# Holding the first four output stores of a convolution until the middle of the third image pair

## The chip, the cores and the metric

The kernel runs on one core of a Trainium2 chip. The metric is the device time of one execution in microseconds (us); the kernel is launched once for the whole computation. Lower is better.

## The reference

A 3x3 convolution with zero padding of 1, stride 1, in fp32, over 16 images of 64 channels and 64 x 64 pixels, to 128 output channels. The weights are given with nine tenths of their values at zero, but the kernel treats them as dense.

```python
def reference(x, weight):               # x (16, 64, 64, 64), weight (128, 64, 3, 3), float32
    ...
    x_pad = np.pad(x, ((0, 0), (0, 0), (pad, pad), (pad, pad)), mode='constant')
    output = np.zeros((batch, c_out, h, w), dtype=np.float32)
    ...
        output[b, co] += weight[co, ci, kh, kw] * x_pad[b, ci, kh:kh+h, kw:kw+w]
    ...
```

The output, 16 x 128 x 64 x 64 floats, is 33.55 MB; the input is 16.78 MB in fp32.

## The kernel before

**Tiling.** The 16 images are taken as 8 pairs. A pair lies on 128 partitions (two images of 64 channels each) as a bf16 tile `xs[p]` of 64 x 64 pixels. One output image is a tile `o` of 128 partitions (its output channels) by 64 x 64 fp32, that is 16 KB for each partition and 2 MB in all. For each pair there are two of them, `o[0]` and `o[1]`.

**Loads.** SyncE issues the load of the weights (L60) and of the upper half of the first pair in fp32 (L62, into a tile of the output pool). GpSimd issues the lower half of the first pair (L63) and the seven other pairs (L67). These eight convert from fp32 to bf16 on the way, so a whole pair writes 1 MB (it reads 2 MB). All are issued within the first 6.2 us, one behind another on GpSimd's queue.

**Compute.** A pair is four blocks of 16 output rows (`blk` 0 to 3). A block goes through `twos` (L151): GpSimd adds neighbouring rows of `xs[p]` into `s` (L154), TensorE forms a shared product of it that ScalarE copies from PSUM to `pc` (L161), TensorE forms a product for the even rows and one for the odd rows (`product`, L121 to L142), and VectorE adds each to `pc` and writes the rows into `o[0]` and `o[1]`: four `tensor_tensor` instructions for each block (L168). The first block of the first pair goes through `direct` (L144) instead.

**Stores.** After the four blocks of a pair SyncE issues its two stores of 2 MB, `o[0]` first (L188). In the last pair it issues stores of half an image (1 MB) after `blk` 1 and after `blk` 3 (L185). So there are 14 stores of 2 MB and four of 1 MB, all on SyncE's queue and in the order of the program; they are called store 0 to store 17 below. SyncE waits at each one until VectorE has written its tile.

**Buffers.** `o_pool` has 7 buffers that are handed out in turn: one to the fp32 half of the first input pair, then two for each output pair. The third pair takes the sixth and the seventh; the fourth pair takes the first (long free) and the second, which held the first pair's `o[0]`. VectorE must therefore see store 0 landed before it writes `o[1]` of the fourth pair, stores 1 and 2 before the fifth pair, stores 3 and 4 before the sixth, and so on.

**Order.** The program is scheduled by hand (`tc.manual_schedule()`), so each engine runs its instructions in the order in which the code writes them. Semaphore waits are derived from what reads and writes the tiles.

Of the kernel before, what the change touches and what calls it, by code (L numbers as in the profile page):

```python
# [27 lines left out]
def kernel(  # L28
# [6 lines left out]
    nc = tc.nc  # L35

    B, C_IN, H, W = x.shape
# [83 lines left out]
    def product(terms, rows):  # L121


        ps = [psum_pool.tile([128, rows, W], FP32, name="ps") for _ in range(2)]
        todo = [(t, kw) for t in terms for kw in KW_ORDER]
        for i, ((src, g, first, step), kw) in enumerate(todo):
            n_src = src.shape[1]
            lo = 0 if first >= 0 else 1
            hi = rows if first + (rows - 1) * step < n_src else rows - 1
            c_lo, c_hi = max(0, 1 - kw), min(W, W + 1 - kw)  # L130
            a = first + lo * step
            b = first + (hi - 1) * step + 1
            for n in range(2):
                q = slice(64 * n, 64 * n + 64)
                nc.tensor.matmul(  # L135
                    ps[n][:, lo:hi, c_lo:c_hi],
                    tap(g, kw, n),
                    src[q, a:b:step, c_lo + kw - 1 : c_hi + kw - 1],
                    start=(i == 0),
                    stop=(i == len(todo) - 1),  # L140
                )
        return ps  # L142

    def direct(p, o, r0, rows):  # L144
        ps = product(
            [(xs[p], G1, r0, 1), (xs[p], G0, r0 - 1, 1), (xs[p], G2, r0 + 1, 1)], rows
        )
        nc.scalar.copy(out=o[0][:, r0 : r0 + rows, :], in_=ps[0])  # L148
        nc.vector.tensor_copy(out=o[1][:, r0 : r0 + rows, :], in_=ps[1])  # L149

    def twos(p, o, r0):  # L151
        t0 = r0 // 2
        s = s_pool.tile([128, 8, W], BF16, name="s")
        nc.gpsimd.tensor_tensor(  # L154
            out=s, in0=xs[p][:, r0 : r0 + 16 : 2, :], in1=xs[p][:, r0 + 1 : r0 + 16 : 2, :], op=ADD
        )
        shared = product([(s, G1, 0, 1)], 8)
        pc = []
        for n in range(2):
            c = p_pool.tile([128, 8, W], FP32, name="pc")  # L160
            nc.scalar.copy(out=c, in_=shared[n])  # L161
            pc.append(c)
        even = [(xs[p], G21, r0 + 1, 2), (xs[p], G0, r0 - 1, 2)]
        odd = [(xs[p], G01, r0, 2), (xs[p], G2, r0 + 2, 2)]
        for first, terms in ((r0, even), (r0 + 1, odd)):
            ps = product(terms, 8)
            for n in range(2):
                nc.vector.tensor_tensor(  # L168
                    out=o[n][:, first : r0 + 16 : 2, :], in0=ps[n], in1=pc[n], op=ADD
                )  # L170

    for p in range(NP):
        o = [o_pool.tile([C_OUT, H, W], FP32, name="o") for _ in range(2)]
        last = p == NP - 1
        for blk in range(4):
            r0 = 16 * blk
            if BLOCKS[p][blk] == "T":
                twos(p, o, r0)
            else:
                for r, rows in ((r0, 8), (r0 + 8, 8)):  # L180
                    direct(p, o, r, rows)
            if last and blk % 2 == 1:
                for n in range(2):
                    rows = slice(r0 - 16, r0 + 16)
                    nc.sync.dma_start(out=out[2 * p + n][:, rows, :], in_=o[n][:, rows, :])  # L185
        if not last:
            for n in range(2):
                nc.sync.dma_start(out=out[2 * p + n], in_=o[n])  # L188


# [28 lines left out]
```

## Time and profile before

| | |
|---|---|
| time, median of 7 runs | 127.67 us |
| lowest and highest of the 7 | 127.62 and 128.13 us |
| the profiled execution's own time | 128.13 us |
| its span in the profile | 126.3 us (126.28 in the trace) |
| DMA moved | 42.93 MB, mean 340 GB/s |
| TensorE busy | 110.3 us (87%) |
| VectorE busy | 82.4 us (65%) |
| GpSimd, ScalarE busy | 40.8 us (32%), 39.0 us (31%) |

The profile is of the slowest of the seven runs: its span is 1.85 us shorter than its time (start and end of the execution lie outside it), and its time is 0.46 us above the median. Times in the text are us from the start of the span. The page cuts the span into 40 slices of 3.16 us; "DMA" is the mean busy share of the 16 DMA engines in tenths, and "GB/s" is what they moved, counted by the bytes written, so that the converting loads appear at half of what they read. "q1 hardware_dynamic" is the queue that SyncE issues on, "q0 software_dynamic" GpSimd's. Under the DMA view the trace holds one record for each packet (start, duration, queue, size). A 2 MB store is 128 packets of 16 KB, eight for each DMA engine, and each engine ends its part with a packet of 4 bytes that raises the semaphore; a store has landed when the last of the 16 has.

### The profile page before, as it was taken

What the parts mean: (1) busy time and instruction counts of PE and PEld (TensorE: products, weight loads), DVE (VectorE), ACT (ScalarE), POOL (GpSimd) and SP (SyncE); (2) the same over time, 40 slices, a digit from 0 to 9 for tenths busy, and PEclk for the clock granted to TensorE, in tenths of its full rate; (3) what the DMA queues carried; (4) which work ended last, traced back from release to release, by engine and by line L of the source; (5) the groups of instructions that cost most, each with busy time, mean ns of one, the idle gap of its engine ahead of it and who ended that gap; (6) DMA issues with size and microseconds to landing.
All of it is one profiled execution on the core that took longest, in us unless ns stands there. A gap on an engine that the chain in (4) does not pass through costs nothing.

```text
span 126.3 us, 2486 instructions
## 1 busy us (share of the span) xinstructions
PE 110.3 (87%) x1002; PEld 56.5 (45%) x1002; DVE 82.4 (65%) x135; ACT 39.0 (31%) x71; POOL 40.8 (32%) x45
## 2 busy tenths in 40 slices
PE   6649999999999999999999999999999999991000
PEld 6414454555455455545554455545554555540000
DVE  0451267787778777877787778777877787776000
ACT  4541232333333333333333333333333333330000
POOL 6909033333333333333333333333333330000000
PEclk9999999999999999999999999999999999999955
DMA  4999999999999999999999999999999979999990
GB/s 114 355 231 210 215 213 213 223 200 252 314 337 298 314 350 301 332 332 413 413 441 441 420 426 415 436 431 418 441 420 426 441 306 426 446 397 407 418 387 23
DMA packets 4044, 42.93 MB, mean 340 GB/s; under 512 B 448, under 2 KB 448, under 8 KB 704
## 3 DMA queue, kind: packets, MB, share of 16 engines
q1 hardware_dynamic: 2880, 34.90, 66.0%
q0 software_dynamic: 1152, 7.86, 30.5%
q8 instruction: 8, 0.13, 0.4%
q14 instruction: 4, 0.03, 0.1%
HBM read 17.07 MB, written 33.55 MB: 401 GB/s over the span
## 4 chain that ended last, share of the span: by engine, by line
PE 83%; DMA 5%; DVE 1%; issue 1%; DVEq 0%; SPq 0%
PE ps L135 83%; DMA o<-in_x_dram 5%; DVE o L168 1%; DVEq L214 0%; DVE x L87 0%; SPq L60 0%; DVEq L168 0%
## 5 line engine op out<-in xcount | busy, mean ns | idle before, releaser
L135 PE MATMUL ps<-x,wT 64*128 64x504 bf16 (+3 forms) x780 | 91.3, 382 | 2.5 <-DVE x L87 2.5
L168 DVE TENSOR_TENSOR o<-ps,pc 128x512 f32<-128x512 f32 x124 | 77.8, 686 | 22.1 <-PE ps L135 19.8
L135 PEld LDWEIGHTS <-wT 64*128 64x128 bf16 x966 | 52.9, 96 | 55.5 <-issue 5.8
L154 POOL TENSOR_TENSOR s<-x 128x512 bf16<-128x512 bf16 x31 | 35.7, 1154 | 61.4 <-PE ps L135 46.4
L161 ACT COPY pc<-ps 128x512 f32<-128x512 f32 x62 | 33.3, 589 | 64.0 <-issue 61.8
L135 PE MATMUL ps<-s,wT 64*128 64x512 bf16 (+1 forms) x186 | 25.5, 377 | 0.0
L149 DVE COPY o<-ps 128x512 f32<-128x512 f32 x2 | 1.4, 692 | 4.7 <-PE ps L135 4.7
L74 PE MATMUL ps<-idle_rhs 128*128 128x128 bf16 x27 | 3.1, 313 | 1.0 <-DVE idle_rhs L71 1.0
L67 POOL DMA_DIRECT2D x<-in_x_dram x7 | 3.7, 560 | 0.0
L74 PEld LDWEIGHTS <-idle_rhs 128*128 128x128 bf16 x27 | 2.8, 149 | 1.0 <-DVE idle_rhs L71 1.0
L91 DVE CAST w_bf<-w_sb 128x192 bf16<-128x192 f32 (+1 forms) x4 | 1.3, 381 | 3.0 <-DMA w_sb<-in_weight_dram 3.0
L148 ACT COPY o<-ps 128x512 f32<-128x512 f32 x2 | 1.2, 586 | 5.2 <-PE ps L135 5.2
L87 DVE CAST x<-o 128x576 bf16<-128x576 f32 x1 | 0.5, 460 | 2.5 <-DMA o<-in_x_dram 2.5
L87 ACT CAST x<-o 128x576 bf16<-128x576 f32 (+1 forms) x2 | 1.5, 802 | 1.5 <-DMA o<-in_x_dram 1.5
L97 PE MATMUL ps<-ident,w_bf 128*128 128x128 bf16 x9 | 1.2, 308 | 0.4 <-DVE w_bf L91 0.4
L91 ACT ACT_TABLE_LOAD x1 | 1.3, 1283 | 0.7 <-PEq L203 0.7
L91 ACT CAST w_bf<-w_sb 128x64 bf16<-128x64 f32 (+1 forms) x2 | 0.7, 417 | 1.9 <-DMA w_sb<-in_weight_dram 1.9
L97 PEld LDWEIGHTS <-w_bf 128*128 128x128 bf16 x9 | 0.8, 130 | 0.8 <-DVE w_bf L91 0.8
L101 DVE TENSOR_TENSOR wT<-ps,wT 128x384 bf16<-128x384 f32 x2 | 1.0, 548 | 0.0
L63 POOL DMA_DIRECT2D x<-in_x_dram x1 | 0.7, 698 | 0.8 <-POOLq L203 0.8
L71 DVE MEMSET idle_rhs<- 128x64 uint32 x1 | 0.1, 112 | 0.8 <-PEq L203 0.8
L110 ACT CAST wT<-ps 128x384 bf16<-128x384 f32 x1 | 0.5, 479 | 0.4 <-PE ps L97 0.4
(8 smaller groups left out, 2.0 us busy)
## 6 DMA issues: line engine op xcount, KB each, us to landing
out_dram<-o SPq DMA_DIRECT2D x14, 2048.0 KB, 16.5
x<-in_x_dram POOLq DMA_DIRECT2D x7, 1024.0 KB, 25.0
out_dram<-o SPq DMA_DIRECT2D x4, 1024.0 KB, 9.4
o<-in_x_dram SPq DMA_DIRECT2D x1, 1024.0 KB, 6.5
x<-in_x_dram POOLq DMA_DIRECT2D x1, 512.0 KB, 7.9
w_sb<-in_weight_dram SPq DMA_DIRECT2D x1, 288.0 KB, 3.1
```

The lines of the kernel that those rows point to most:

```text
L67: nc.gpsimd.dma_start(out=xs[p], in_=pair(p))
L74: nc.tensor.matmul(idle_ps, idle_rhs, idle_rhs, start=True, stop=True)
L87: copy(out=xs[0][:, a:b, :], in_=x_head[:, a:b, :])
L91: copy(out=w_bf4[:, g, a:b, :], in_=w_v[:, k : k + b - a, :])
L97: nc.tensor.matmul(wps[:, j, :], src, ident, start=True, stop=True)
L101: nc.vector.tensor_tensor(out=wT[:, g], in0=wps, in1=wT[:, G1], op=SUB)
L135: nc.tensor.matmul(ps[n][:, lo:hi, c_lo:c_hi], tap(g, kw, n), src[q, a:b:step, c_lo + kw - 1 : c_hi + kw - 1], start=(i == 0), stop=(i == ...
L148: nc.scalar.copy(out=o[0][:, r0 : r0 + rows, :], in_=ps[0])
L149: nc.vector.tensor_copy(out=o[1][:, r0 : r0 + rows, :], in_=ps[1])
L154: nc.gpsimd.tensor_tensor(out=s, in0=xs[p][:, r0 : r0 + 16 : 2, :], in1=xs[p][:, r0 + 1 : r0 + 16 : 2, :], op=ADD)
L161: nc.scalar.copy(out=c, in_=shared[n])
L168: nc.vector.tensor_tensor(out=o[n][:, first : r0 + 16 : 2, :], in0=ps[n], in1=pc[n], op=ADD)
```

## The change

The stores of the first two pairs (stores 0 to 3, `HELD = 2`) are not issued after their pairs. They are kept in a list, and are issued in a row after `blk` 1 of the third pair. Store 0 is given a dependency on the last VectorE instruction of that block (`done`, which `twos` now returns); stores 1 to 3 follow it on SyncE's queue and have nothing more to wait for. All later stores stay where they were. The stores go through a helper `store`, which changes nothing in them. No instruction on TensorE, VectorE, ScalarE or GpSimd is added, removed or moved, and SyncE has the same 18 stores in the same order: only the wait ahead of store 0 differs, and stores 1 to 3 come free with it.

```diff
             for n in range(2):
-                nc.vector.tensor_tensor(
+                done = nc.vector.tensor_tensor(
                     out=o[n][:, first : r0 + 16 : 2, :], in0=ps[n], in1=pc[n], op=ADD
                 )
+        return done
+
+    HELD = 2
+    held = []
+
+    def store(p, n, o, a, b):
+        return nc.sync.dma_start(out=out[2 * p + n][:, a:b, :], in_=o[n][:, a:b, :])
...
             if BLOCKS[p][blk] == "T":
-                twos(p, o, r0)
+                done = twos(p, o, r0)
...
             if last and blk % 2 == 1:
                 for n in range(2):
-                    rows = slice(r0 - 16, r0 + 16)
-                    nc.sync.dma_start(out=out[2 * p + n][:, rows, :], in_=o[n][:, rows, :])
-        if not last:
+                    store(p, n, o, r0 - 16, r0 + 16)
+            if p == HELD and blk == 1:
+                first = store(*held[0])
+                tc.add_manual_dep(
+                    first.ins,
+                    done.ins.name,
+                    mybir.DependencyInfo(
+                        mybir.DependencyClass.Sync, mybir.DependencyReason.DATA
+                    ),
+                    reason="loads first",
+                )
+                for args in held[1:]:
+                    store(*args)
+        if p < HELD:
+            held += [(p, n, o, 0, H) for n in range(2)]
+        elif not last:
             for n in range(2):
-                nc.sync.dma_start(out=out[2 * p + n], in_=o[n])
+                store(p, n, o, 0, H)
```

## The prediction

> **What bounds the kernel now.** I read the chain of waits first. It gives TensorE 83% of the span, and it would make the change harmless, since no instruction of TensorE moves. But the last work of TensorE ends at 114.2 and VectorE's at 115.5, while the span is 126.28. So I read the rows of the page on the DMA engines next.
>
> ```profile
> PE   6649999999999999999999999999999999991000
> ...
> DMA  4999999999999999999999999999999979999990
> GB/s 114 355 231 210 215 213 213 223 200 252 314 337 298 314 350 301 332 332 413 413 441 441 420 426 415 436 431 418 441 420 426 441 306 426 446 397 407 418 387 23
> ...
> q1 hardware_dynamic: 2880, 34.90, 66.0%
> q0 software_dynamic: 1152, 7.86, 30.5%
> ```
>
> The engines are busy in every slice from the second to the 39th, with one dent (the 33rd, 306 GB/s, at 101 to 104). The two queues together take 96.5% of 16 engines' span. There are three phases: loads alone at about 215 GB/s up to 28; loads and stores in turn at 300 to 350 up to 57; stores alone at 413 to 441 after that. The windows say the same: a DMA share of 1.0 or slightly more in the long stretches (neighbouring packets overlap a little).
>
> ```profile
> 8.00:28.00 20.00, 19.82 (x162) 9.51 (x163) 11.91 (x21) 6.64 (x12) 7.98 (x7) 1.00 1.05 216
> 30.00:57.00 27.00, 27.00 (x256) 13.59 (x254) 21.44 (x35) 8.59 (x16) 9.24 (x8) 1.00 1.02 322
> 58.00:100.00 42.00, 42.00 (x397) 21.12 (x394) 32.66 (x52) 14.30 (x27) 15.35 (x14) 1.00 1.01 428
> 100.00:104.00 4.00, 4.00 (x42) 2.10 (x40) 3.16 (x6) 1.08 (x3) 1.35 (x2) 1.00 0.81 340
> ```
>
> The last two columns are the DMA share and GB/s. Next I asked the DMA view for single stores, by a window around the issue of each; the last column is us from issue to landing. Here are stores 0, 3, 5, 9, 11, 12 (issued at 25.40, 38.74, 51.55, 77.16, 89.96, 102.17):
>
> ```profile
> out_dram<-o SPq DMA_DIRECT2D x1, 2048.0 KB, 15.7
> out_dram<-o SPq DMA_DIRECT2D x1, 2048.0 KB, 26.2
> out_dram<-o SPq DMA_DIRECT2D x1, 2048.0 KB, 23.1
> out_dram<-o SPq DMA_DIRECT2D x1, 2048.0 KB, 17.2
> out_dram<-o SPq DMA_DIRECT2D x1, 2048.0 KB, 14.7
> out_dram<-o SPq DMA_DIRECT2D x1, 2048.0 KB, 7.6
> ```
>
> The stores stand in a backlog that shrinks from 26 us to 7.6. Is it gone at 102.17, so that compute sets the end? On most engines, yes; on one, no. The packet records show 14 or 15 engines passing from one 2 MB store to the next in 4.862 us (eight 16 KB packets of 0.611). They run dry between 101.5 and 103.1, and that is the dent. One engine, A from here on, needs 5.165 in the stores-only phase (packets of 0.634 to 0.660). The 4-byte packets that end its part stand at 88.664, 93.840, 98.988, 104.165, 109.323, 114.471. Store 12 was issued at 102.17, so A never waits for work. It ends at 124.72, the other engines mostly at 122.9, and store 17 lands at 125.13. So what sets the end is engine A, busy without a pause since the first loads. Any time in which A stands still is added to the kernel; TensorE has slack beside it.
>
> **The change part by part.**
>
> *When the held stores start.* The release is the last VectorE instruction of block 1 of the third pair:
>
> ```profile
> 42.55 2.52 DVE L168 TENSOR_TENSOR o<-ps,pc 128x512 f32<-128x512 f32 x4 [0.73 <-PE ps L135]
> 45.79 2.51 DVE L168 TENSOR_TENSOR o<-ps,pc 128x512 f32<-128x512 f32 x4 [0.73 <-PE ps L135]
> 49.03 2.48 DVE L168 TENSOR_TENSOR o<-ps,pc 128x512 f32<-128x512 f32 x4 [0.73 <-PE ps L135]
> ```
>
> The third pair's `o[0]` is issued at 50.95, within the last row, so the last row is block 3 and the first is block 1: it ends at 45.07. SyncE issues 0.10 later (as at 25.40, after a tile done at 25.30), at 45.17. From issue to first packet the rings need 0.83 where they are empty (store 12: 102.17 to 103.00) and 4.06 where loads stand in front (store 0 today: 25.40 to 29.46). I take 0.83, because the loads are over by then (next step): first packet at 46.00. With 1.01, as at the weights' load (0.74 to 1.75), it would be 46.18.
>
> *When the loads end.* Alone on the engines, one pair takes 4.867 us of each (4-byte packets of one engine at 12.766, 17.633, 22.500). The third of the 1 MB loads ends between 22.50 and 23.66, depending on the engine; four more take 19.47 and end between 41.97 and 43.13. No engine has anything to do from then until 46.00: 2.9 to 4.0 us of standstill, where today there is none. This is the cost of the change.
>
> *What the separation gives back.* Today four loads and three stores (x 4.867 + 4.862 = 34.05 in all) take A and its peers from 22.5 to 23.7 up to 57.7 to 59.1, 35.3: 1.2 too long, most of it around 27 to 29.5, where load packets take 0.7 to 1.4 instead of 0.624. That 1.2 is saved. But beside loads A's store packets took 0.624 like all others', and its extra 0.3 for each store shows only where stores are alone. In the changed kernel stores 0 to 2 are alone too: 3 x 0.303 = 0.9 comes back as a loss on A.
>
> *The sum on A.* Three stores end at 46.00 + 3 x 5.165 = 61.50; today A has ended store 2 at 57.72. From there on its work is the same: 3.78 later to the end, 128.50, landing at 128.91. On the other engines: 46.00 + 14 x 4.862 + 4 x 2.45 = 123.9, or 124.8 at the 4.93 that a 2 MB store takes after the restart at 103 (107.92 to 112.85), so they don't set the end.
>
> *Who waits for the later landing.* VectorE needs store 0 for the second instruction of the fourth pair, at 52.11 + 0.63 = 52.74. Store 0 would end on A at 51.17 and land 0.37 later, at 51.5 (today the last 4-byte packet is at 40.73 and the landing at 41.10): 1.2 of margin, so it costs nothing. The fifth pair, at about 65, needs stores 1 and 2 (61.9), the sixth, at 77.7, stores 3 and 4 (72.2), the seventh, at 90.5, stores 5 and 6 (82.5): free as well. Without that cover, a landing late by d stalls VectorE by d less 1.2, and TensorE a little later when PSUM is full; even then A has work until 108, 6 us past the time when stores 12 and 13 are issued, so a stall of up to 5 us of TensorE wouldn't reach the end. Behind the waiting store on SyncE's queue are only stores 1 to 3, free with it, and stores 4 and 5, whose tiles are ready at 50.95 and later. GpSimd's loads were all issued by 6.2. No queue is held up that someone else waits on.
>
> *Two rules against rows.* The Trainium skill, "DMA: Bandwidth & Descriptors", in "Anatomy of one DMA", gives the time of a transfer as 2.0 us plus its bytes at 436 GB/s (a fit for GpSimd's path). By this estimate the 33.55 MB of stores end at 45.17 + 2.0 + 77.0 = 124.2, 1.0 before today's landing; the trace has 5.165 for 2 MB on the engine that ends last, where this rule has 4.81, and the trace decides. The same page, in "Latency and other measured facts", says that engines 7 and 15 are usually slower, with GpSimd's descriptor rings as the best guess and as a matter of that path alone. Here the slow engine is slow from 58 to 114, when GpSimd's queue moves nothing, and not while it loads; if the rule did hold, A would lose nothing on stores and the end would be that of the other engines.
>
> **The rivals.** (1) *Forecast: standstill plus A's pace*: +3.78. The profiled span becomes 130.06 and its time 131.91; the median of the seven runs is 0.46 below the profiled one, so 131.45, given as 131.4. (2) *A's slowness is not of stores alone but of today's mix* and it runs like the rest. Then the end is that of 16 equal engines: 46.00 + 14 x 4.862 + 4 x 2.45 + 0.41 = 124.3 at the fast pace, 0.8 before 125.13, that is 126.8 and faster; at 4.93 for a store it is 125.2, no change, 127.8. It decides if a 2 MB store costs A less than (125.13 - 0.41 - 46.00 - 10.25) / 14 = 4.89 (10.25 is A's time for the last four today). Against it: eleven stores at 5.13 to 5.18 in a row, through dent and restart; for it: its packets were normal in the mix and nearly so in the last 1 MB stores (2.45). (3) *A loses less*: 5.0 for a store gives 2.3 less on 14, +1.5, 129.1. (4) *The restart is slow* or store 0 lands too late: 4.06 instead of 0.83 adds 3.2, 134.6; only loads in front of it explain the 4.06, so little is left for it. (5) *The change doesn't do what it says*: if the wait were passed earlier, the stores would start among the loads as today and the time would be 127.7.
>
> **How the numbers follow.** A measurement of this kernel can tell about 0.2% (0.26 us) from no change. Forecast 0.78 (130.4 to 132.2, from an A of 5.10 to 5.18 and a start 0.2 earlier or later); (3) 0.12, spread over 128.1 to 130.4; (2) 0.06, split between faster 0.03 and same 0.03; (4) 0.03; (5) 0.01, same. So faster 0.03, same 0.04, slower 0.93. The range leaves out the lower half of (3), (2), (5) and (4): 129.3 to 132.4.
>
> **What would show it.** In the changed profile: the slices near 42 to 46 fall well below 9 in the DMA row, with q0 empty after about 43.5; 215 GB/s up to there; no slice at 300 to 350; no dent at 101 to 104; the 4-byte packets of one engine 5.1 to 5.2 apart from the first store on; VectorE's idle time and TensorE's end (114.2) unchanged; store 17 landing near 128.9. It would be wrong if all 16 engines end together near 124, if the loads run past 45, or if VectorE waits on a DMA in the fourth pair.

## The result and the profile after

| | before | after |
|---|---|---|
| median | 127.68 us (34 runs) | 129.29 us (13 runs) |
| lowest and highest | 127.10 and 130.03 | 127.60 and 130.61 |
| profiled execution: time, span | 128.13, 126.28 | 129.51, 127.7 |

The change makes the kernel slower: the ratio is 1.0092, with a 95% interval of 1.0068 to 1.0116. The ratio leaves out runs over 1.5% above the fastest of their kernel, five of the change's among them, so it is smaller than that of the medians (1.0126, 1.61 us); the runs of the change spread over 3 us, and why they do is part of the explanation. The forecast of 131.4 had the direction right and the size more than twice too large, and the median lies 0.01 us under the range.

The rows of the page on TensorE, the DMA engines and the two queues, for the changed kernel (a slice is 3.19 us):

```profile
PE   6569999999999999999999999999999999920000
...
DMA  4999999999999499999999999999999999999970
GB/s 133 342 223 213 218 218 215 210 218 221 210 213 218 131 410 410 410 472 410 413 410 421 462 416 410 416 418 441 421 421 421 416 446 426 421 392 418 426 313 18
...
q1 hardware_dynamic: 2880, 34.90, 65.4%
q0 software_dynamic: 1152, 7.86, 29.6%
```

The middle phase at 300 to 350 GB/s is gone: loads alone up to the 13th slice, at 210 to 223 from the third on, then stores alone. Between them stands one slice at 131 GB/s and a busy share of 4, and the dent before the last stores is gone. The windows put the standstill in place; the last two columns are the DMA share and GB/s:

```profile
42.00:43.00 1.00, 1.00 (x12) 0.57 (x10) 1.00 (x3) 0.11 (x1) 0.01 (x1) 1.00 0.26 57
43.00:44.40 1.40, 1.40 (x18) 0.70 (x13) 0.67 (x2) 0.97 (x2) 1.15 (x1) 1.00 0.00 0
44.40:46.00 1.60, 1.60 (x18) 0.88 (x16) 1.60 (x3) 0.00 (x0) 0.00 (x0) 1.00 1.18 492
```

The timeline shows the start of TensorE's real work, the block that releases the stores, and the release:

```profile
7.66 5.67 PE L135 MATMUL ps<-x,wT 64*128 64x512 bf16 x36 [2.51 <-DVE x L87]
...
40.97 2.52 DVE L168 TENSOR_TENSOR o<-ps,pc 128x512 f32<-128x512 f32 x4 [0.73 <-PE ps L135]
...
43.58 3.09 SPq L179 DMA_DIRECT2D out_dram<-o  x4
```

Block 1 of the third pair ends at 43.49, not 45.07, and SyncE issues store 0 at 43.58; the packet records have the first store packet at 44.42. The answers of the DMA view for store 0 (43.58) and store 12 (issued at 100.60):

```profile
out_dram<-o SPq DMA_DIRECT2D x1, 2048.0 KB, 6.4
...
out_dram<-o SPq DMA_DIRECT2D x1, 2048.0 KB, 11.3
```

Store 0 lands in 6.4 us instead of 15.7, since no loads stand in front of it. Store 12 needs 11.3 instead of 7.6: at its issue more of the earlier stores still stand in front of it. The last store lands at 126.60.

### The profile page after: what moved, and what is told of

The parts are those of the page before. It is cut to its first block, busy times and chain, and to the rows that moved or that the text cites. A ratio compares the mean times of both kernels' runs of the same rounds, so it can differ in the third digit from the quotient of the medians.

```text
span 127.7 us, 2486 instructions
## 1 busy us (share of the span) xinstructions
PE 108.9 (85%) x1002; PEld 58.8 (46%) x1002; DVE 82.3 (64%) x135; ACT 39.0 (31%) x71; POOL 40.8 (32%) x45
## 4 chain that ended last, share of the span: by engine, by line
PE 81%; DMA 5%; DVE 1%; issue 1%; DVEq 0%; SPq 0%
PE ps L135 81%; DMA o<-in_x_dram 5%; DVE o L168 1%; DVEq L236 0%; DVE x L87 0%; SPq L60 0%; DVEq L168 0%
## 5 line engine op out<-in xcount | busy, mean ns | idle before, releaser
L135 PEld LDWEIGHTS <-wT 64*128 64x128 bf16 x966 | 55.4, 95 | 51.8 <-issue 4.1
```

The costliest lines, as they stand in the source:

```text
L135: nc.tensor.matmul(ps[n][:, lo:hi, c_lo:c_hi], tap(g, kw, n), src[q, a:b:step, c_lo + kw - 1 : c_hi + kw - 1], start=(i == 0), stop=(i == ...
```

## Experiments

In the packet records I read two numbers for each kernel: the first store packet, and the landing of the last store. Theory "standstill" is the forecast's: the time is the release plus what the slow DMA engine needs for all stores, and only the standstill costs.

**Release after block 0.**

```diff
-            if p == HELD and blk == 1:
+            if p == HELD and blk == 0:
```

> The held stores are released after block 0 of the third pair instead of block 1. In the profile of the change block 0 ends 3.24 us before block 1, at about 40.4, while the loads end on the engines between 42.0 and 43.5. Theory standstill (the DMA engines stood still from 42.0-43.5 to 44.4, and the time is the release plus the stores on the slowest engine): no engine stands still, so the time falls by the 1.0 to 2.4 us of the standstill, to 126.9-128.3, about the kernel before (127.7) or a little under it; the DMA row of the page has no slice below 9 at 40 to 46. Rival pace (what costs is that stores run alone, so that one engine needs 5.14 us for each where it needed 4.99 beside loads): a release 3.2 us earlier changes hardly anything in that, the stores still run almost alone, and the time stays within 0.5 us of 129.3.

Measured: median 127.50 us (12 runs, 127.10 to 128.37), ratio to before 0.9987 (0.9969 to 1.0006). The rows of its page:

```profile
DMA  4999999999999999999999999999999999999960
GB/s 138 344 227 214 208 216 216 222 216 214 208 216 216 334 425 433 417 433 427 440 417 438 417 422 443 427 433 420 422 422 443 396 427 433 427 388 420 422 261 13
```

No slice below 9, and the loss is gone, while loads and stores are nearly as separate as in the change: the rate goes from 216 GB/s to 425 with a single mixed slice, of 334, between them. So it isn't the separation that costs.

**Release after block 2.**

```diff
-            if p == HELD and blk == 1:
+            if p == HELD and blk == 2:
```

> The held stores are released after block 2 of the third pair, 3.24 us later than in the change, at about 46.8. Theory standstill: the end follows the release one for one, 129.3 + 3.2 = 132.5 us. Store 0 then lands at about 47.7 + 5.14 + 0.4 = 53.2 where VectorE needs it at 51.2, so VectorE stalls for 2 us on a DMA in the fourth pair and TensorE ends up to 2 us later, without any further effect on the end because the stores have a backlog. Rival compute (the end is set by the fourth pair being held up, or by the last stores being issued late): the end follows the stall of VectorE only, about +2 us over a kernel with no stall, 130 to 131.5. Rival pace: under 0.5 us of change, 129.3 to 129.8.

Measured: median 131.87 us (6 runs, 130.44 to 132.96), ratio 1.0285 (1.0235 to 1.0334). That is 2.6 us over the change's median, not the full 3.2; the release of the profiled execution was at 44.76, only 1.18 after that of the change's profile, since its first 36 matmuls ended 2.06 earlier (they started at 7.28 and took 3.99, where the change's started at 7.66 and took 5.67), and that execution took 130.51, 1.00 more than the change's. What VectorE waited for, and its timeline at the fourth pair:

```profile
DVE o L168 <- DMA out_dram<-o: 2.8, 2, 2.1
```

```profile
48.48 0.69 DVE L168 TENSOR_TENSOR o<-ps,pc 128x512 f32<-128x512 f32 x1 [0.60 <-PE ps L135]
51.30 6.67 DVE L168 TENSOR_TENSOR o<-ps,pc 128x512 f32<-128x512 f32 x11 [2.14 <-DMA out_dram<-o]
```

The second instruction of the pair waits 2.14 us for store 0, which landed at 51.18. It then catches up with eleven instructions in a row, and VectorE ends at 112.30, before the change's 113.97. The stall is there and costs nothing at the end, as the backlog covers it.

**One store not held.**

```diff
         if p < HELD:
-            held += [(p, n, o, 0, H) for n in range(2)]
+            if p == 0:
+                store(p, 0, o, 0, H)
+            held += [(p, n, o, 0, H) for n in range(2) if (p, n) != (0, 0)]
```

> Store 0 is issued after the first pair as in the kernel before; stores 1 to 3 are held as in the change. Store 0 gives each DMA engine 4.9 us of work among the loads, so the loads end at about 47-48.5 instead of 42.0-43.5, past the release at 43.6. Theory standstill: no engine stands still, and the time falls by 1.0 to 2.4 us, to 126.9-128.3. Rival pace: stores 1 to 17 still run without loads beside them but for the first, so at most 0.3 us is saved and the time is 129.0-129.3. If stores among loads cost more than they save (in the kernel before, loads and three stores took 1.2 us longer together than one by one), the time is nearer 128.3 than 126.9.

Measured: median 128.03 us (12 runs, 127.73 to 128.35), ratio 1.0025 (1.0010 to 1.0040). The loads end between 49.1 and 52.6, no slice of the DMA row between the first and the 39th is below 9, and most of the loss is gone. What is left, 0.3 us, is at the end of the interval that the expectation gave to loads and stores costing more together.

**Stores cut in halves.** In the kernel before:

```diff
             for n in range(2):
-                nc.sync.dma_start(out=out[2 * p + n], in_=o[n])
+                for a in (0, H // 2):
+                    b = a + H // 2
+                    nc.sync.dma_start(out=out[2 * p + n][:, a:b, :], in_=o[n][:, a:b, :])
```

> The kernel before, with each 2 MB store issued as two of 1 MB (32 rows, 8 KB for each partition) at the same place; nothing held. In the kernel before the end is that of one DMA engine that takes 5.165 us for a 2 MB store where the others take 4.862, but 2.45 for each of the last 1 MB stores. Theory of the packet (its slow pace belongs to packets of 16 KB): the engine takes 4.9 for 2 MB too, all engines run dry near 102, and the end is that of the last stores after their issue, about 1.0 to 1.8 us earlier: 126 to 126.7 us. Rival place (that engine is slow on stores whatever their packets): no change, 127.4 to 127.9; the last stores were quick for another reason. A loss would say that the doubled number of issues or of semaphore waits on SyncE costs something: each is some 0.35 us of SyncE, and SyncE is far from full.

Measured: median 128.44 us (6 runs, 128.26 to 128.49), ratio 1.0054 (1.0033 to 1.0075). That is above the intervals of both theories. The theory of the packet falls: one DMA engine still ends at 124.86 where the next one ends at 123.3, and its packets of 8 KB take 0.324 to 0.347 where the others' take 0.31. The edit also does more than was meant: a half is issued as soon as its own rows are written, so the first store goes out at 17.13 (25.40 and 24.52 in the two profiles of the kernel before). More of the stores then share the engines with the loads, and there the rate is lower:

```profile
GB/s 131 345 223 220 212 210 199 290 285 272 293 269 298 277 290 285 277 401 422 419 425 437 412 425 435 419 419 430 419 425 432 417 422 432 422 417 430 430 290 10
```

269 to 298 GB/s in the mixed slices, against 298 to 350 in the kernel before, but over a longer stretch. How much of the 0.5% comes from this isn't separated here.

**Wait for the last load.**

```diff
-        nc.gpsimd.dma_start(out=xs[p], in_=pair(p))
+        loads[p] = nc.gpsimd.dma_start(out=xs[p], in_=pair(p))
...
                 tc.add_manual_dep(
                     first.ins,
-                    done.ins.name,
+                    loads[7].ins.name,
```

The held stores are issued from the place after block 0, so that nothing but the load and their own tiles is waited for.

> The held stores wait for the landing of the last load (eighth pair) instead of VectorE's block; nothing else differs from the change. The last load lands at 43.7 in the profiles, whatever TensorE does, so the release is at about 43.8 and the first store packet at 44.6; the engines whose loads end first (42.0) stand still for 2.6 us, the last (43.4) for 1.2. Theory standstill, with the release of the change riding on TensorE's start (first 36 matmuls 3.99 to 6.72 us in five profiles): the median is near the change's, 129.3 to 129.8, but the runs of the change lie from 127.6 to 130.6 and these lie within about 1 us of one another. Rival spread (the change's runs spread because of the slow DMA engine or the HBM, not of the release): the runs here spread by 2 to 3 us as well.

Measured: median 129.73 us (4 runs, 129.62 to 129.85), ratio 1.0157 (1.0143 to 1.0171). Who SyncE waited for:

```profile
SPq L180 <- DMA x<-in_x_dram: 42.0, 1, 42.0
```

It is the same loss as in the change, but the spread of 3 us has shrunk to 0.23, though over four runs only. The stores and the loads are the same in both; only the release no longer rides on compute.

**Wait for the load before the last.** As above, with `loads[6]`.

> The held stores wait for the landing of the load of the seventh pair (38.9 in the profiles), one load before the end; release about 39.0, first packets among those of the last load, no standstill. Theory standstill: 127.1 to 127.9, like the release after block 0 (127.5), that is about the kernel before. Rival pace: 129 to 129.5, since nearly all stores still run alone.

Measured: median 127.73 us (11 runs, 127.52 to 129.28), ratio 1.0012 (0.9988 to 1.0037): no loss. SyncE issues store 0 at 39.18, and the first store packet follows the first load's end on an engine, at 42.15, without a gap.

**A cold start, in both kernels.**

```diff
-    for _ in range(27):
+    for _ in range(1):
         nc.tensor.matmul(idle_ps, idle_rhs, idle_rhs, start=True, stop=True)
```

> The kernel before with one idle matmul at its start instead of 27, so that TensorE's first matmuls run slower and all compute comes later by some d, estimated at 1 to 2 us from the 3.99 to 6.72 us that the first 36 matmuls took in the profiles. Theory standstill: the DMA engines have a backlog from 29 to the end, so a later compute does not move the time until the slow engine runs dry: 127.5 to 128.2. Rival compute (TensorE, which the chain of waits names with 83%, sets the end): +d, 128.7 to 129.7.

> The change with one idle matmul at its start instead of 27, so that its release comes later by the same d of 1 to 2 us as in the kernel before without them. Theory standstill: the time moves one for one with the release, 129.3 + d = 130.3 to 131.3, while the kernel before does not move. Rival pace: no move, 129.3. Rival compute: both kernels move by d.

Measured: before, cold: 127.70 us (10 runs), ratio 1.0000 (0.9987 to 1.0013). The change, cold: 129.99 us (4 runs), ratio 1.0174 (1.0148 to 1.0199). The edit turned out weak: the first 36 matmuls took 5.84 and 6.39 us in the two profiles. In the kernel before compute came no later at all: block 1 of the third pair ended at 43.53 in the cold profile and at 45.07 in the first one. So the 127.70 says nothing about a later compute. In the change the release moved by only 0.52 (to 44.10), and the time of the profiled execution moved with it, from 129.51 to 130.03. The medians differ by 0.70, well inside the 3 us over which the runs of the change spread. So the sign of the theory is there, but not the 1 to 2 us that I had expected, and this pair is weak evidence.

**A warm start, in both kernels.**

```diff
+    for _ in range(20):
+        nc.tensor.matmul(idle_ps, idle_rhs, idle_rhs, start=True, stop=True)
     cast_x(nc.scalar.copy, 9, 18)
```

> The change with 20 more idle matmuls on TensorE between the transposes of the weights and the first product, where TensorE has some 2.5 us of idle time, so that the first 36 matmuls run at the 3.99 us of one profile (the change's own needed 5.67). All compute, and with it the release, should come 1.7 us earlier, at about 41.9 instead of 43.6, while the loads end at 42.0-43.4 as before. Theory standstill: the time falls by 1.2 to 1.7 us to 127.6-128.1, with runs within about 1 us of one another. Rival pace: no move, 129.3. If the idle matmuls run past the arrival of the first input, the start comes later by that and less is gained.

> The kernel before with the same 20 idle matmuls. Theory standstill: compute ends about 1.7 us earlier and the time does not move, 127.5 to 127.9, because the slow DMA engine is busy without a pause from the first load on. Rival compute: the time falls by 1 to 1.7 us, to 126-126.7.

Measured: the change, warm: median 127.80 us (12 runs; 11 of them between 127.53 and 127.91, one at 132.05), ratio 0.9995 (0.9976 to 1.0014). The timeline of TensorE:

```profile
5.64 1.34 PE L116 MATMUL ps<-idle_rhs 128*128 128x128 bf16 x20
7.63 3.99 PE L137 MATMUL ps<-x,wT 64*128 64x512 bf16 x36 [0.66 <-DVE x L87]
```

and its DMA row:

```profile
DMA  4999999999999999999999999999999999999970
```

The first 36 matmuls take 3.99 instead of 5.67; the release comes at 41.87, the first store packet at 42.72, and both the loss and the spread are gone, although no line of the change was touched. This is the cleanest of the experiments: the same stores in the same order behind the same dependency cost nothing once the release meets the end of the loads. The kernel before, warm: 127.48 us (12 runs), ratio 0.9978 (0.9959 to 0.9996). The rival's 126 to 126.7 is out; a gain of 0.2% that I had not expected is left, at the edge of what can be told. In that profile the first 36 matmuls took 4.94, and block 1 of the third pair ended at 43.07, 2.00 before that of the first profile of the kernel before; the last store landed at 124.75, 0.38 before.

**The kernel before again.**

> The kernel before once more, for a second profile of it. Theory standstill (with the profile shown first being a late start): the third pair's block 1 ends at 43 to 44 instead of 45.1, the first 36 matmuls need 5.7 or less instead of 6.72, and the last store still lands at 124.6 to 125.2, with one DMA engine ending 1 to 2 us after the others. If the block ends at 45.1 again, the forecast's release was right for the kernel before and the change itself moved it.

Measured: 127.81 us (one run). TensorE's first matmuls, in the profile shown first and then in this one:

```profile
8.18 6.72 PE L135 MATMUL ps<-x,wT 64*128 64x512 bf16 x36 [2.48 <-DVE x L87]
```

```profile
7.42 6.59 PE L135 MATMUL ps<-x,wT 64*128 64x512 bf16 x36 [1.59 <-DVE x L87]
...
41.67 2.52 DVE L168 TENSOR_TENSOR o<-ps,pc 128x512 f32<-128x512 f32 x4 [0.73 <-PE ps L135]
```

Block 1 of the third pair, the last row, ends at 44.19 here, 0.88 earlier than in the first profile though 0.2 after the 43 to 44 expected, and the last store lands at 124.89, 0.24 earlier. The start differs between executions of one kernel, and the end of the kernel before hardly follows it. The duration of 36 matmuls was expected at 5.7 or less and is 6.59: part of this one's earlier block comes from the first input's earlier arrival (its cast starts at 6.91, not 7.66).

**Both cures at once.** Release after block 0, and the 20 idle matmuls.

> Both edits that took the standstill away: the held stores are released after block 0 of the third pair, and TensorE has the 20 more idle matmuls before the first product. Theory standstill: no engine stands still from the first load to the end, and the time is that of the slow engine's whole work, 127.1 to 127.6, with runs within about 1 us; the two gains do not add up, since the standstill can go only once (release after block 0 alone: 127.5; idle matmuls alone: 127.8). If the gains did add up, 126 to 126.3.

Measured: median 127.96 us (12 runs, 127.25 to 129.31), ratio 1.0019 (1.0005 to 1.0034). The gains don't add up, as expected, but the median is 0.4 above the interval's end, and no run here says why: the profiled execution, at 127.45, lies inside the interval, and its last store landed at 124.44, earlier than in any other profile. No version here beats the kernel before by more than 0.2%.

## Why the prediction was right and where it failed

The relation at its core, that the end follows the first store packet one for one, can be read from the profiles of the five kernels in which the stores start alone:

| kernel | release issued | first store packet | last landing | difference | time of that execution |
|---|---|---|---|---|---|
| change, warm | 41.87 | 42.72 | 124.89 | 82.17 | 127.82 |
| change | 43.58 | 44.42 | 126.60 | 82.18 | 129.51 |
| wait for the last load | 43.70 | 44.55 | 126.71 | 82.16 | 129.62 |
| change, cold | 44.10 | 44.95 | 127.12 | 82.17 | 130.03 |
| release after block 2 | 44.76 | 45.60 | 127.60 | 82.00 | 130.51 |

- *What bounds the kernel*: right. The slow engine ends last in all the profiles. In four profiles of the kernel before (two as it is, one cold, one warm) block 1 of the third pair ended anywhere from 43.07 to 45.07, 2.0 apart, and the last landing stayed within 0.4 (124.75 to 125.13). The chain of waits, with TensorE at 81% of the span, points at the wrong engine in the changed kernel too.
- *When the held stores start*: **this step failed.** I took the release from the one profiled execution, at 45.17 with 46.00 for the first packet, and gave it 0.2 us either way. It was 43.58 and 44.42: 1.58 less. The delay from issue to first packet was right (0.84 for 0.83). What was wrong is the compute before it: that execution's first matmuls started 0.52 later and took 6.72 us where the change's took 5.67, so that they ended 1.57 later, and over all profiles here those 36 matmuls took from 3.99 to 6.72. The change itself didn't move compute: from the end of those matmuls to the end of block 1 of the third pair it is 30.17 and 30.18 in the two profiles of before and 30.16 in the change. TensorE's end, which I had expected unchanged at 114.2, came at 112.6, earlier by the same 1.57. For the kernel before this is hidden; for the change it is the release. I had seen that the profiled execution was the slowest of the seven, and used it only to take 0.46 off the total, not to doubt its start.
- *When the loads end*: right: 41.97 to 43.13 forecast, 41.99 to 43.45 measured. The standstill is then 1.0 to 2.4 us where 2.9 to 4.0 was forecast.
- *The stores on engine A*: nearly right, and the second term that was mis-sized. From the first store packet to the last landing I had 82.91; it is 82.18. The 14 stores of 2 MB took 71.90 on A, 5.136 each, where the forecast's rows make 72.24 (0.34 less: the third to the thirteenth took 5.15 to 5.19 each, the last only 4.98). The last four of 1 MB took 9.81 for 10.25: the 10.25 held one step of 2.89 us, which none of the other profiles of the kernel before has. The landing came 0.47 after A's end instead of 0.41.
- *What the separation gives back*: agrees in sum. I had 1.2 back and 0.9 lost on A, 0.3 net; the kernels with separate phases and no standstill land their last store at 124.61 and 124.67 against 125.13 and 124.89 in the two profiles of before. By the times this isn't resolved (0.9987 with 0.9969 to 1.0006). Against the 124.61 of the release after block 0 the change's last landing is 1.99 later: that is what the standstill cost by these profiles, within the 1.0 to 2.4.
- *Who waits for store 0*: right. It landed at 49.96 and was needed at 51.2, a margin of 1.2 us as forecast; with the release 1.18 later VectorE stalled 2.14 us, without effect on the end.

With the two mis-sized terms the sum closes: 3.78 - 1.58 - 0.73 = 1.47, and the last landing moved by 126.60 - 125.13 = 1.47. From the median of before, 127.67 + 1.47 = 129.14 against 129.29 measured. Rivals (2), (4) and (5) are refuted: A did not run like the other engines, store 0 was not held up at restart, and the wait took place. Rival (3) had 129.1, close to the measured 129.29, but by luck: it asked for 5.0 us for a store on A, which was 5.136, and kept the release at 45.17.

The spread fits the same step. With the release on compute, the runs lie from 127.60 to 130.61; on a load's landing, within 0.23 us (four runs); with a warm start, 11 of 12 within 0.38. Each kernel has one trace, so for the other runs this is inferred from their times. Why the first matmuls take now 3.99 us and now 6.72 stays open.

## What to carry to other kernels

Where the DMA engines are the bound, as here, a dependency that holds transfers back must end before the last earlier transfer does; each us of standstill went into the time in full, and the margin has to cover the start's scatter. Tie such a release to the transfers themselves (a load before the last one) rather than to compute, so that it doesn't inherit the scatter of TensorE's start (with the wait for the load before the last, 10 of 11 runs lay within 0.61 us). And when an edit makes something wait on an event that was hidden before, look at how that event moves between executions, not only at its place in one profile.

## What the runs showed of the hardware

- With no loads beside it and while TensorE ran, one DMA engine of 16 took 5.14 to 5.19 us for a 2 MB store where the others mostly took 4.86 to 4.95, and with it set the end of every version: 0.2 to 0.3 us for each store. Its slow packets (0.64 to 0.66 us for 16 KB, 0.324 to 0.347 for 8 KB) stop within 1.5 us before TensorE stops: at 110.6 in the release after block 2, where TensorE's matmuls end at 111.1; at 112.2 in the kernel with halves (112.4); at 111.3 in the change (112.6); at 112.1 in the wait for the last load (112.5); at 113.8 before (114.2). After that a 2 MB store took 4.86 on it as well (the last one of release after block 2: from 112.45 to 117.31). So it was neither the packet's size nor the fewer rows that made the last stores quick. What slows that engine wasn't tried, and that its slow packets end close to TensorE's last matmul doesn't show TensorE to be the cause: beside loads, with TensorE running too, the engine wasn't slow (in the kernel before, 62 of 1093 store packets from 58 to 100 took 0.632 to 0.67 us, and one of 357 from 30 to 57).
- The first 36 matmuls of a program with 27 idle ones ahead took 3.99 to 6.72 us from one execution to the next, with granted clocks between 0.50 and 1.00 in the windows at 7 to 13; in the slowest (6.72) the records show a granted clock of 1.00 throughout, so the granted clock alone doesn't tell it. With 20 more idle matmuls right ahead of the product, the two profiles of kernels that hold the stores had 3.99, and the kernel before had 4.94.
